# A two-layer hybrid token mixer on one core: scan products moved from GpSimd to VectorE, Mamba step sizes multiplied in at the outputs, and the last norm moved ahead of a branch

## The chip, the cores and the metric

The kernel runs on one core of a Trainium2 chip. The metric is device time in microseconds (us), from the start of one execution to its end. Five engines work beside each other, each with an instruction stream of its own that is executed in order: TensorE (PE, matrix products, with its weight loads shown as PEld), VectorE (DVE), ScalarE (ACT), GpSimd (POOL) and SyncE (SP), which here only issues DMA transfers. An instruction starts when those ahead of it on its engine have started or ended and the semaphores that it waits for have come.

## What is computed

256 latent and 256 context tokens of width 1024 pass through two layers. In each layer a normed and modulated input goes through one projection into three mixers that run side by side, a diagonal state-space scan (S5), a gated delta rule (GDN) and Mamba-2 (SSD), each in both directions; their outputs are concatenated and projected back. Then comes a dense SwiGLU (layer 0) or a top-2-of-8 mixture of experts (layer 1), and after layer 1 a last RMSNorm. The parts of the reference that the change touches, cut:

```python
# S5: h_t = lam * h_(t-1) + bu_t, complex, both directions
def _affine_combine(left, right):
    a_l, b_l = left
    a_r, b_r = right
    return a_l * a_r, a_r * b_l + b_r
# Mamba-2 inside a chunk: xdt = x * dt, and exp(cs_i - cs_j) for i >= j
y_diag = jnp.einsum("bncge,bnsge,bgjncs,bnsgjp->bncgjp", cc, bc, seg_decay(a_cs), xc)
y_off = jnp.einsum("bncge,bngjpe,bgjnc->bncgjp", cc, states[:, :-1], jnp.exp(a_cs))
...
y = xf * lax.rsqrt(jnp.mean(xf * xf, axis=-1, keepdims=True) + EPS)   # rmsnorm
```

## The kernel before

All matrix products of fp32 operands are made of three products of rounded parts: an operand is split into a high part H (ACT, line 321 for weights) and a remainder L (DVE, line 322), and PE sums hH·wH, hL·wH and hH·wL. So each weight tile costs a transfer, one ACT and one DVE instruction before PE can use it.

The source issues work in the order of the functions, and a scheduler then sets the order on each engine from priority bands (`self.band(...)`, with the numbers of the tables `Q0` for layer 0 and `Q1` for layer 1) and from the reuse of buffers in the pools. On the chip that order is fixed: an instruction that waits holds up all behind it on its engine, and a DMA that waits holds up all behind it on the SP queue.

In the mixer of a layer, the input projection runs on PE, and its tiles pass a convolution of four multiply-adds on DVE (`cv_acc`, line 800). Beside it stand, on DVE and POOL, the S5 scan (`s5_scan`: 11 levels over the 64 steps of the state `s5B`; for each piece two products `s5t` on POOL, line 609, and two additions on DVE, line 612), the remainders `wL` of the weights that are loaded, the GDN preparation (`gd_x`, `gd_prod`, and the iteration `iv_Q`, `iv_X` of lines 940 and 943) and the Mamba decays (`m2_decays`).

`m2_decays` makes, for four heads and one block of 128 tokens at a time (a quad; 16 quads in layer 0, 8 in layer 1), a 128x128 matrix for each head. `decay_quad` takes two `affine_select` on POOL (line 776), products on PE and one Exp on ACT (line 781), which give the decay `dq_W`. Lines 1070 and 1071 build `dq_E` = le·dt0 + ge·dt1 from the two triangles le and ge and the step sizes of the two directions, with one ACT and one DVE instruction for each head, POOL multiplies it with `dq_W` (line 1072), and line 1073 stores it to the scratch `WD` in DRAM. Later `m2` loads the matrices back as `m_E` (line 1161), multiplies them with the product B·C of that group from PSUM (line 1162) and uses them as moving operands on PE (`outs`, 12 calls in both layers together, two quads in each). The states of `m2` and the carried-in parts `m_yo` share one ring of buffers (`m2_xe`). `gate` norms the output (`m_sq`, `m_z`) and stores it to `yD`, from where `out_proj` reads it (`yr`, split into `yo`).

After the scan, `s5X` is stored to the scratch `XD` (line 626), on the same SP queue as the stores to `WD` and the loads for `m2`.

In the mixture of experts the main path computes all experts with up to 128 tokens each. `moe_rest` is a branch for experts with more tokens than that (a count `cnt` is loaded into registers on every engine, and the branch is not taken with these inputs). After the branch stands `final`, the last norm: squares on ACT, a sum over the features as eight products with a matrix of ones on PE, the reciprocal root (`rs_h`, `rs_y`, `rs_t`, `fr`), eight products `fy` shared out between DVE and POOL, and four DMAs.

Of the kernel before, what the change touches and what calls it, by code (L numbers as in the profile page):

```python
# [90 lines left out]
class Net:  # L91
# [968 lines left out]
    def m2_decays(self, p, sm, WD, first):  # L1060

        nc = self.nc
        for h0 in (0, 4, 8, 12):
            for t in range(first, 4):
                W = p.tile([128, 4, 128], F32, name="dq_W", bufs=2)
                self.decay_quad(p, sm, t, h0, W, "bg", 2)
                E = p.tile([128, 4, 128], F32, name="dq_E", bufs=2)
                for h in range(4):
                    dt = [sm["sp"][:, t, d * 20 + h0 + h:d * 20 + h0 + h + 1] for d in range(2)]
                    nc.scalar.activation(E[:, h], self.ge, AF.Copy, scale=dt[1])  # L1070
                    nc.vector.scalar_tensor_tensor(E[:, h], self.le, dt[0], E[:, h], op0=OP.mult, op1=OP.add)
# [923 lines left out]
```

## Time and profile before

| | before |
|---|---|
| time, median of 3 runs | 2540.91 us (2539.93 to 2543.95) |
| the profiled execution | 2542.29 us |
| its span in the trace | 2540.6 us |
| mean granted TensorE clock | 0.958 |
| PE busy | 2327.2 us (92%) |
| DVE busy | 1887.3 us (74%) |
| ACT busy | 1422.5 us (56%) |
| POOL busy | 377.0 us (15%) |

The profile is of one execution. Busy time is the time in which an engine executes instructions other than register, branch and DMA-issuing ones; it is an average over the whole span, in which the engines take turns at being the slowest. The 1.7 us between the execution's time and its span lie outside of the trace.

### The profile page before, as it was taken

What the parts mean: (1) busy time and instruction counts of PE and PEld (TensorE: products, weight loads), DVE (VectorE), ACT (ScalarE), POOL (GpSimd) and SP (SyncE); (2) the same over time, 40 slices, a digit from 0 to 9 for tenths busy, and PEclk for the clock granted to TensorE, in tenths of its full rate; (3) what the DMA queues carried; (4) which work ended last, traced back from release to release, by engine and by line L of the source; (5) the groups of instructions that cost most, each with busy time, mean ns of one, the idle gap of its engine ahead of it and who ended that gap; (6) DMA issues with size and microseconds to landing.
All of it is one profiled execution on the core that took longest, in us unless ns stands there. A gap on an engine that the chain in (4) does not pass through costs nothing. (4 is left out here: it accounts for less than half of the span.)

```text
span 2540.6 us, 36281 instructions
## 1 busy us (share of the span) xinstructions
PE 2327.2 (92%) x12886; PEld 1873.5 (74%) x12886; DVE 1887.3 (74%) x3035; ACT 1422.5 (56%) x2203; POOL 377.0 (15%) x435
## 2 busy tenths in 40 slices
PE   7999786889989999998988789789999999999997
PEld 4878665666757777886876667787887888888876
DVE  8787998446558674436578975568888888888886
ACT  4665476333234444235756653447777777676765
POOL 0011667312100000000046442100000000000000
PEclk9899997999989999998998899889999999999998
DMA  7444332986445656323443445387999999999993
GB/s 248 125 126 122 101 102 90 267 268 224 145 170 206 245 164 215 92 93 95 151 139 110 157 148 158 112 294 271 346 340 339 350 341 338 358 340 342 346 354 133
DMA packets 222378, 543.86 MB, mean 214 GB/s; under 512 B 25584, under 2 KB 105456, under 8 KB 186096
## 3 DMA queue, kind: packets, MB, share of 16 engines
q1 hardware_dynamic: 222192, 541.49, 62.0%
q8 instruction: 103, 1.69, 0.3%
q14 instruction: 83, 0.68, 0.1%
HBM read 487.87 MB, written 53.54 MB: 213 GB/s over the span
## 5 line engine op out<-in xcount | busy, mean ns | idle before, releaser
L1670 DVE TENSOR_TENSOR mwL<-mwr,mwH 128x2048 fp32r<-128x2048 f32 (+1 forms) x272 | 605.0, 2226 | 97.2 <-PE bank L162 59.1
L1669 ACT ACTIVATE mwH<-mwr 128x2048 fp32r<-128x2048 f32 (+1 forms) x272 | 508.1, 1868 | 204.6 <-PE bank L162 168.6
L321 ACT ACTIVATE wH<-wr 128x512 fp32r<-128x512 f32 (+2 forms) x388 | 233.1, 605 | 380.2 <-PE bank L162 261.5
L322 DVE TENSOR_TENSOR wL<-wr,wH 128x512 fp32r<-128x512 f32 (+2 forms) x388 | 279.9, 724 | 210.1 <-ACT wH L321 202.7
L162 PE MATMUL bank<-mwL,xeH 128*128 128x512 f32 (+1 forms) x768 | 292.6, 381 | 9.3 <-DVE mwL L1670 9.3
L162 PE MATMUL bank<-mwH,xeL 128*128 128x512 f32 (+1 forms) x768 | 288.1, 376 | 0.0
L162 PE MATMUL bank<-mwH,xeH 128*128 128x512 f32 (+1 forms) x768 | 284.7, 377 | 1.7 <-ACT mwH L1669 1.7
L162 PE MATMUL bank<-hH,wH 128*128 128x512 f32 (+2 forms) x656 | 249.1, 387 | 28.3 <-ACT cv_acc L798 15.2
L162 PE MATMUL bank<-hH,wL 128*128 128x512 f32 (+2 forms) x656 | 250.5, 382 | 14.3 <-DVE wL L322 14.3
L162 PE MATMUL bank<-hL,wH 128*128 128x512 f32 (+2 forms) x656 | 250.8, 383 | 1.1 <-DVE hL L300 1.1
L800 DVE SCALAR_TENSOR_TENSOR cv_acc<-cv_raw,pp,cv_acc 128x512 f32<-128x512 f32 (+1 forms) x192 | 164.9, 874 | 11.1 <-ACT cv_acc L796 5.8
L162 PEld LDWEIGHTS bank<-mwL,xeH 128*128 128x128 f32 x768 | 144.3, 188 | 37.7 <-DVE mwL L1670 11.7
L162 PEld LDWEIGHTS bank<-hH,wH 128*128 128x128 f32 (+1 forms) x656 | 127.2, 195 | 56.6 <-ACT cv_acc L798 17.1
L162 PEld LDWEIGHTS bank<-mwH,xeH 128*128 128x128 f32 x768 | 144.1, 188 | 31.5 <-ACT mwH L1669 2.5
L162 PEld LDWEIGHTS bank<-mwH,xeL 128*128 128x128 f32 x768 | 144.3, 188 | 26.2
L162 PEld LDWEIGHTS bank<-hH,wL 128*128 128x128 f32 (+1 forms) x656 | 127.8, 195 | 40.4 <-DVE wL L322 16.9
L162 PE MATMUL bank<-yo,wH 128*128 128x512 f32 (+1 forms) x512 | 134.0, 353 | 16.2 <-ACT yo L1385 12.1
L162 PEld LDWEIGHTS bank<-hL,wH 128*128 128x128 f32 (+1 forms) x656 | 127.7, 195 | 25.4 <-DVE hL L300 2.4
L162 PE MATMUL bank<-mwL,eaH 128*128 128x512 f32 x352 | 139.2, 396 | 0.0
L162 PE MATMUL bank<-fhH,wH 128*128 128x512 f32 x352 | 138.1, 396 | 0.9 <-ACT fa L1439 0.9
L162 PE MATMUL bank<-mwH,eaL 128*128 128x512 f32 x352 | 138.5, 394 | 0.0
L162 PE MATMUL bank<-fhL,wH 128*128 128x512 f32 x352 | 138.0, 392 | 0.0
(447 smaller groups left out, 4684.2 us busy)
## 6 DMA issues: line engine op xcount, KB each, us to landing
mwr<-in_moe_gu_dram SPq DMA_DIRECT2D x176, 1024.0 KB, 6.3
mwr<-in_moe_dn_dram SPq DMA_DIRECT2D x80, 1024.0 KB, 6.3
wr<-in_w_in_dram SPq DMA_DIRECT2D x160, 256.0 KB, 2.9
ada<-in_ada_w_dram SPq DMA_DIRECT2D x24, 1024.0 KB, 6.4
wr<-in_w_out_dram SPq DMA_DIRECT2D x64, 256.0 KB, 2.8
ada<-in_ada_w_dram SPq DMA_DIRECT2D x32, 512.0 KB, 6.5
wr<-in_ffn_w_gate_dram SPq DMA_DIRECT2D x44, 256.0 KB, 2.7
wr<-in_ffn_w_up_dram SPq DMA_DIRECT2D x44, 256.0 KB, 2.7
```

The costliest lines, as they stand in the source:

```text
L162: return self.nc.tensor.matmul(*a, **k)
L321: nc.scalar.activation(wH, w, AF.Copy)
L322: nc.vector.tensor_tensor(wL, w, wH.bitcast(F32), op=OP.subtract)
L800: nc.vector.scalar_tensor_tensor(acc, raw[:, :, j:j + 256], w[:, j:j + 1], acc, op0=OP.mult, op1=OP.add)
L1669: nc.scalar.activation(wH, w, AF.Copy)
L1670: nc.vector.tensor_tensor(wL, w, wH.bitcast(F32), op=OP.subtract)
```

## The change

It has three parts. In `s5_scan` the products move from POOL to DVE. `m2_decays` stops after the Exp and stores `dq_W` itself, with four buffers instead of two; `outs` takes over what it left out: B·C from PSUM is masked with le and ge into two SBUF tiles (which reuse the slices of B and C in `m_in`), and for each head ACT scales one with dt1, DVE adds the other times dt0, and DVE multiplies a quad with the loaded `m_W`. The product of B and C now stands behind the carried-in parts, and the quads `m_E` come from the ring `m2_xe`, which has five buffers instead of four. The last norm is called ahead of the branch, on tiles that the expert pool has already, with all eight products on DVE and a DMA behind every second one; inside the branch it is called once more.

```diff
@@ s5_scan
-                    nc.gpsimd.tensor_tensor(t[x], src[:, :, ::-1, :] if x else src,
+                    nc.vector.tensor_tensor(t[x], src[:, :, ::-1, :] if x else src,
                                             lam[:, e, x].unsqueeze(1).to_broadcast([128, m, 2, 32]), op=OP.mult)
@@ m2_decays
-                W = p.tile([128, 4, 128], F32, name="dq_W", bufs=2)
+                W = p.tile([128, 4, 128], F32, name="dq_W", bufs=4)
                 self.decay_quad(p, sm, t, h0, W, "bg", 2)
-                E = p.tile([128, 4, 128], F32, name="dq_E", bufs=2)
-                for h in range(4):
-                    dt = [sm["sp"][:, t, d * 20 + h0 + h:d * 20 + h0 + h + 1] for d in range(2)]
-                    nc.scalar.activation(E[:, h], self.ge, AF.Copy, scale=dt[1])
-                    nc.vector.scalar_tensor_tensor(E[:, h], self.le, dt[0], E[:, h], op0=OP.mult, op1=OP.add)
-                nc.gpsimd.tensor_tensor(E, E, W, op=OP.mult)
-                nc.sync.dma_start(WD[:, t, h0:h0 + 4], E)
+                nc.sync.dma_start(WD[:, t, h0:h0 + 4], W)
@@ m2, outs: behind the carried-in parts
-            psc = bank()
-            self.mm(psc[:, 0:128], BT, CT, start=True, stop=True)
...
+            psc = bank()
+            self.mm(psc[:, 0:128], BT, CT, start=True, stop=True)
+
+            nc.vector.tensor_tensor(BT, psc[:, 0:128], self.le, op=OP.mult)
+            nc.vector.tensor_tensor(CT, psc[:, 0:128], self.ge, op=OP.mult)
             E = []
             for q in range(2):
-                E.append(p.tile([128, 4, 128], F32, name="m2_E", bufs=Q[l]["b_E"]))
                 h0 = g * 8 + 4 * q
-                nc.sync.dma_start(E[q], WD[:, t, h0:h0 + 4])
-                nc.vector.tensor_tensor(E[q], psc[:, 0:128].unsqueeze(1).to_broadcast([128, 4, 128]), E[q], op=OP.mult)
+                W = p.tile([128, 4, 128], F32, name="m2_W", bufs=Q[l]["b_E"] - 1)
+                nc.sync.dma_start(W, WD[:, t, h0:h0 + 4])
+                E.append(p.tile([128, 4, 128], F32, name="m2_E", tag="m2_xe", bufs=Q[l]["b_xe"] + 1))
+                for h in range(4):
+                    dt = [sm["sp"][:, t, d * 20 + h0 + h:d * 20 + h0 + h + 1] for d in range(2)]
+                    nc.scalar.activation(E[q][:, h], CT, AF.Copy, scale=dt[1])
+                    nc.vector.scalar_tensor_tensor(E[q][:, h], BT, dt[0], E[q][:, h], op0=OP.mult, op1=OP.add)
+                nc.vector.tensor_tensor(E[q], E[q], W, op=OP.mult)
@@ moe, at its end
+        last = self.final_tiles(px[1][0], acc)
+        self.final(*last)
+        self.moe_rest(l, ab, ht, rk, gate, iota, cnt, last)
         px[1][1].close()
-        self.moe_rest(l, ab, ht, rk, gate, iota, cnt)
@@ final, new
+        for k in range(KT):
+            nc.scalar.activation(sq[:, k], self.xT[:, k], AF.Square)
+            self.mm(ps[:, :256], self.ones, sq[:, k], start=(k == 0), stop=(k == KT - 1))
+        self.rsqrt(None, r, ps[:, :256], [128, 256], 1.0 / D, tiles=tiles)
+        g = self.prm(0, "fng")
+        for k in range(KT):
+            nc.vector.scalar_tensor_tensor(y[:, k], self.xT[:, k], g[:, k:k + 1], r, op0=OP.mult, op1=OP.mult)
+            if k % 2 == 1:
+                nc.sync.dma_start(self.out.rearrange("(k p) t -> p k t", p=128)[:, k - 1:k + 1], y[:, k - 1:k + 1])
```

The order on the engines is the scheduler's, so it is shown here at three places, first of before and then of the change. A row is one instruction, or several alike in a row (xN).

The first place is DVE at the start of the scan of layer 0 (`s5B` the scan's additions, `s5t` its products, `cv_acc` the convolution, `wL` the remainders of weights, `gd_x` GDN's preparation). Before:

```order
L892 TENSOR_TENSOR gd_x_2930<-gd_x_2930,gd_prod_3080 128x16x15
L800 SCALAR_TENSOR_TENSOR cv_acc<-cv_raw,pp_72,cv_acc 128x512
L612 TENSOR_TENSOR s5B<-s5B,s5t 128x8x64 x2
L322 TENSOR_TENSOR wL<-wr,wH 128x512
L612 TENSOR_TENSOR s5B<-s5B,s5t 128x8x64
L800 SCALAR_TENSOR_TENSOR cv_acc<-cv_raw,pp_72,cv_acc 128x512
L612 TENSOR_TENSOR s5B<-s5B,s5t 128x8x64
L800 SCALAR_TENSOR_TENSOR cv_acc<-cv_raw,pp_72,cv_acc 128x512
L322 TENSOR_TENSOR wL<-wr,wH 128x512
L892 TENSOR_TENSOR gd_x_2935<-gd_x_2935,gd_prod_3085 128x16x15
L800 SCALAR_TENSOR_TENSOR cv_acc<-cv_raw,pp_72,cv_acc 128x512
L612 TENSOR_TENSOR s5B<-s5B,s5t 128x8x64
```

Of the change:

```order
L892 TENSOR_TENSOR gd_x_2930<-gd_x_2930,gd_prod_3080 128x16x15
L609 TENSOR_TENSOR s5t<-s5B,s5l 128x512 x3
L800 SCALAR_TENSOR_TENSOR cv_acc<-cv_raw,pp_72,cv_acc 128x512
L609 TENSOR_TENSOR s5t<-s5B,s5l 128x512
L892 TENSOR_TENSOR gd_x_2935<-gd_x_2935,gd_prod_3085 128x16x15
L612 TENSOR_TENSOR s5B<-s5B,s5t 128x8x64 x2
L322 TENSOR_TENSOR wL<-wr,wH 128x512
L800 SCALAR_TENSOR_TENSOR cv_acc<-cv_raw,pp_72,cv_acc 128x512
L612 TENSOR_TENSOR s5B<-s5B,s5t 128x8x64
L609 TENSOR_TENSOR s5t<-s5B,s5l 128x512
L612 TENSOR_TENSOR s5B<-s5B,s5t 128x8x64
L609 TENSOR_TENSOR s5t<-s5B,s5l 128x512
```

The products stand in pairs ahead of the additions that read them, among the same convolution steps and remainders.

The second place is the SP queue in layer 0 behind the scan (`WD` the store of a quad, `XD` that of the scan's result, `m_in` and `m_E` the first loads of `m2`, `ada` the modulation weights, whose source is the same size each time). Before:

```order
L1073 DMA WD_3090<-dq_E 128x512
L626 DMA XD_1897<-s5X 128x512
L1073 DMA WD_3090<-dq_E 128x512
L626 DMA XD_1897<-s5X 128x512 x4
L1073 DMA WD_3090<-dq_E 128x512
L626 DMA XD_1897<-s5X 128x512 x3
L1073 DMA WD_3090<-dq_E 128x512
L1161 DMA m_E<-WD_3090 128x512 x4
L1101 DMA m_in<-mD_94 128x4x128
L1103 DMA m_in<-mD_94 128x2x128
L1101 DMA m_in<-mD_94 128x4x128
L1103 DMA m_in<-mD_94 128x2x128
```

Of the change, from the last stores to `WD` on:

```order
L1067 DMA WD_3090<-dq_W 128x512 x3
L1335 DMA mD_94<-cvo 128x512
L1067 DMA WD_3090<-dq_W 128x512
L190 DMA ada<-in_ada_w_dram 128x4x256 x2
L1067 DMA WD_3090<-dq_W 128x512
L190 DMA ada<-in_ada_w_dram 128x4x256
L626 DMA XD_1897<-s5X 128x512
L190 DMA ada<-in_ada_w_dram 128x4x256
L626 DMA XD_1897<-s5X 128x512 x2
L190 DMA ada<-in_ada_w_dram 128x4x256
L626 DMA XD_1897<-s5X 128x512
L1335 DMA mD_94<-cvo 128x512
```

The last stores of quads stood among and behind those to `XD`, and now all 16 stand ahead of the first of these; loads of `ada` have come to stand between the stores to `XD`, and the first loads of `m2` stand 25 rows further down the queue than before.

The third place is PE in the output projection of layer 0 (`yo` its operand, `m_E` and `m_yo` the last outputs of `m2`, `m_sq` the sum of squares of its last `gate`). Before, the last `m_sq`:

```order
L162 MATMUL bank_6905<-yo,wH 128x512 x2
L162 MATMUL bank_6905<-yo,wL 128x512
L162 MATMUL bank_6905<-yo,wH 128x512 x2
L162 MATMUL bank_7001<-yo,wH 128x512 x2
L162 MATMUL bank_6905<-yo,wL 128x512
L162 MATMUL bank_6594<-m_sq,cst 128x256 x4
L162 MATMUL bank_7001<-yo,wL 128x512
L162 MATMUL bank_7001<-yo,wH 128x512 x2
L162 MATMUL bank_7001<-yo,wL 128x512
```

Of the change:

```order
L162 MATMUL bank_7040<-yo,wL 128x512
L162 MATMUL bank_7040<-yo,wH 128x512 x2
L162 MATMUL bank_7040<-yo,wL 128x512
L162 MATMUL bank_6538<-m_S_6293,m_in 128x512
L162 MATMUL bank_6571<-m_E,m_xt 64x128 x8
L162 MATMUL bank_6571<-cst,m_yo 128x128 x4
L162 MATMUL bank_6594<-m_sq,cst 128x256 x4
L162 MATMUL bank_6962<-yo,wH 128x512
L162 MATMUL bank_7001<-yo,wH 128x512
L162 MATMUL bank_7040<-yo,wH 128x512
L162 MATMUL bank_6962<-yo,wH 128x512
```

Of the 384 products with `yo`, 206 stood ahead of the last `m_sq`, and now 228 do; the last `m_E` and `m_yo`, which stood 138 instructions or more ahead of it, now stand directly before it.

## Rows read from the trace of the kernel before

**Rows 1.** The page: busy time by engine; DVE busy tenths in 40 slices.
```profile
PE 2327.2 (92%) x12886; PEld 1873.5 (74%) x12886; DVE 1887.3 (74%) x3035; ACT 1422.5 (56%) x2203; POOL 377.0 (15%) x435
...
DVE  8787998446558674436578975568888888888886
```

**Rows 2.** Busy time by stretch: us, each engine, TensorE clock, DMA share.
```profile
430.00:480.00 50.00, 39.46 (x265) 30.01 (x263) 27.11 (x48) 35.85 (x81) 23.52 (x22) 0.86 0.67 208
480.00:530.00 50.00, 40.97 (x348) 29.11 (x344) 26.04 (x55) 13.59 (x37) 16.18 (x15) 0.96 0.97 279
...
1500.00:1580.00 80.00, 73.43 (x568) 58.30 (x567) 42.89 (x83) 24.02 (x60) 19.80 (x17) 1.00 0.61 170
1760.00:2500.00 740.00, 729.76 (x3510) 601.79 (x3509) 641.45 (x410) 535.67 (x398) 0.00 (x0) 1.00 0.93 345
```

**Rows 3.** DVE by group, 283 to 417 us: xcount | busy, mean ns | idle.
```profile
L800 DVE SCALAR_TENSOR_TENSOR cv_acc<-cv_raw,pp,cv_acc 128x512 f32<-128x512 f32 x42 | 48.1, 1151 | 0.1
L612 DVE TENSOR_TENSOR s5B<-s5B,s5t 128x512 f32<-128x512 f32 x20 | 25.5, 1279 | 0.1
L1071 DVE SCALAR_TENSOR_TENSOR dq_E<-cst,sp,dq_E 128x128 f32<-128x128 f32 x36 | 23.1, 685 | 0.0
L322 DVE TENSOR_TENSOR wL<-wr,wH 128x512 fp32r<-128x512 f32 x19 | 22.9, 1210 | 0.0
...
L940 DVE TENSOR_TENSOR iv_Q<-bank,cst 128x512 f32<-128x512 f32 x8 | 5.3, 677 | 0.0
```

**Rows 4.** POOL by group, the same stretch.
```profile
L609 POOL TENSOR_TENSOR s5t<-s5B,s5l 128x512 f32<-128x512 f32 x22 | 35.6, 1634 | 8.5 <-DVE s5B L612 8.5
L776 POOL TENSOR_SCALAR_AFFINE_SELECT dq_r<-la 128x1024 fp32r<-128x1024 f32 x20 | 28.1, 1415 | 0.6 <-PE bank L162 0.6
L1072 POOL TENSOR_TENSOR dq_E<-dq_E,dq_W 128x512 f32<-128x512 f32 x9 | 13.9, 1550 | 4.7 <-ACT dq_W L781 3.2 <-issue 1.4
```

**Rows 5.** Timeline of DVE around 1320 us: start, duration (of all xN).
```profile
1317.82 3.44 DVE L322 TENSOR_TENSOR wL<-wr,wH 128x512 fp32r<-128x512 f32 x2
...
1323.28 0.68 DVE L612 TENSOR_TENSOR s5B<-s5B,s5t 128x512 f32<-128x512 f32 x1
1323.88 0.68 DVE L322 TENSOR_TENSOR wL<-wr,wH 128x512 fp32r<-128x512 f32 x1
```

**Rows 6.** Timeline of POOL at the same time.
```profile
1313.94 6.77 POOL L609 TENSOR_TENSOR s5t<-s5B,s5l 128x512 f32<-128x512 f32 x4
```

**Rows 7.** Timeline of DVE at 462 us, POOL quiet.
```profile
462.30 1.17 DVE L1071 SCALAR_TENSOR_TENSOR dq_E<-cst,sp,dq_E 128x128 f32<-128x128 f32 x4 [0.28 <-ACT dq_E L1070]
```

**Rows 8.** Timeline of DVE at 451 us; in brackets its idle time before.
```profile
451.21 0.61 DVE L1071 SCALAR_TENSOR_TENSOR dq_E<-cst,sp,dq_E 128x128 f32<-128x128 f32 x2 [8.46 <-issue]
```

**Rows 9.** Timeline of the SP queue at 442 us.
```profile
442.79 6.74 SPq L626 DMA_DIRECT2D XD<-s5X  x3
```

**Rows 10.** ACT by group, 283 to 435 us: the scalings of the decays.
```profile
L1070 ACT ACTIVATE dq_E<-cst,sp 128x128 f32<-128x128 f32 x44 | 14.1, 400 | 20.8 <-DMA WD<-dq_E 11.0 <-DVE gd_x L892 9.7
```

**Rows 11.** DVE by group, layer 1, 1299 to 1437.5 us.
```profile
L322 DVE TENSOR_TENSOR wL<-wr,wH 128x512 fp32r<-128x512 f32 x45 | 43.3, 969 | 13.0 <-ACT wH L321 13.0
...
L612 DVE TENSOR_TENSOR s5B<-s5B,s5t 128x512 f32<-128x512 f32 x22 | 25.5, 1167 | 0.1
```

**Rows 12.** DVE, the decay matrices of layer 1, 1300 to 1500 us.
```profile
L1071 DVE SCALAR_TENSOR_TENSOR dq_E<-cst,sp,dq_E 128x128 f32<-128x128 f32 x32 | 18.8, 637 | 0.0
```

**Rows 13.** PE waits of 640 to 770 us: total, times, longest.
```profile
PE bank L162 <- ACT yo L1385: 7.9, 1, 7.9
```

**Rows 14.** Timeline of the tail, three of its rows.
```profile
2518.30 3.22 DVE L1773 SCALAR_TENSOR_TENSOR xT<-bank,mods,xT 128x256 f32<-128x256 f32 x8
...
2521.60 2.56 ACT L1865 ACTIVATE fsq<-xT 128x256 f32<-128x256 f32 x8 [2.34 <-DVEq L1779]
...
2524.18 6.49 PE L162 MATMUL bank<-fsq,cst 128*128 128x256 f32 x16 [4.23 <-ACT fsq L1865]
```

**Rows 15.** Busy time by stretch, where the last norm sums its squares.
```profile
2524.00:2528.00 4.00, 3.82 (x9) 3.15 (x10) 0.00 (x0) 2.64 (x5) 0.00 (x0) 0.50 0.02 4
```

More of the change, by code (lines that the diff above doesn't have):

```diff
@@ L1118, in states @@
                         continue
-                    w = p.tile(s8, F32, name="m2_xe", tag="m2_xe", bufs=Q[l]["b_xe"])
+                    w = p.tile(s8, F32, name="m2_xe", tag="m2_xe", bufs=Q[l]["b_xe"] + 1)
                     nc.vector.tensor_tensor(w, v8(px), hb(sm["dde"][:, d, t, hs]), op=OP.mult)
@@ L1617, in gather @@
         nc = self.nc
-        xH, xL = [p.tile([128, KT, 2, 128], F32R, name=f"xe{x}") for x in "HL"]
+        xH, xL = [p.tile([128, KT, 2, 128], F32R, name=f"xe{x}", tag=f"xe{x}") for x in "HL"]
         yield xH, xL
@@ L1773, in moe_add, with moe_rest @@
         self.nc.vector.scalar_tensor_tensor(x, y, self.mods[l][:, 40 + m, 0:1], x, op0=OP.mult, op1=OP.add)
-    def moe_rest(self, l, ab, hts, rk, gate, iota, cnt):
+    def moe_rest(self, l, ab, hts, rk, gate, iota, cnt, last):
         nc, tc, A = self.nc, self.tc, self.A
@@ L1837, in moe_rest @@
                             nc.vector.tensor_tensor(sg, pg[1], sg, op=OP.mult)
-                            wd = p.tile([128, D], F32, name="r_wd", bufs=2)
+                            wd = p.tile([128, D], F32, name="r_wd")
                             for half in range(2):
@@ L1845, in moe_rest @@
                                         stop=(f == FF // 128 - 1))
-                        yv = p.tile([128, D], F32, name="r_yv")
+                        yv = p.tile([128, D], F32, name="r_yv", tag="r_xe")
                         for half in range(2):
@@ L1857, in moe_rest, with final_tiles, final @@
                         nc.vector.tensor_scalar(ec, ec, 1.0, None, op0=OP.add)
-    def final(self):
-        nc, tc = self.nc, self.tc
-        with tc.tile_pool(name="fin", bufs=1) as p:
-            ps = self.ps("mm")
-            for k in range(KT):
-                sq = p.tile([128, 256], F32, name="fsq", bufs=KT)
-                nc.scalar.activation(sq, self.xT[:, k], AF.Square)
-                self.mm(ps[:, :256], self.ones, sq, start=(k == 0), stop=(k == KT - 1))
-            r = p.tile([128, 256], F32, name="fr")
-            self.rsqrt(p, r, ps[:, :256], [128, 256], 1.0 / D)
-            y = p.tile([128, KT, 256], F32, name="fy")
-            g = self.prm(0, "fng")
-            xg = p.tile([128, 3, 256], F32, name="fxg")
-            for i in range(3):
-                nc.scalar.activation(xg[:, i], self.xT[:, 2 * i + 1], AF.Copy, scale=g[:, 2 * i + 1:2 * i + 2])
-            for k in range(KT):
-                if k in (1, 3, 5):
-                    nc.gpsimd.tensor_tensor(y[:, k], xg[:, k // 2], r, op=OP.mult)
-                else:
-                    nc.vector.scalar_tensor_tensor(y[:, k], self.xT[:, k], g[:, k:k + 1], r, op0=OP.mult, op1=OP.mult)
-            for k0 in range(0, KT, 2):
-                nc.sync.dma_start(self.out.rearrange("(k p) t -> p k t", p=128)[:, k0:k0 + 2], y[:, k0:k0 + 2])
+            self.final(*last)
+    def final_tiles(self, p, acc):
+        y = p.tile([128, KT, 256], F32, name="fy", tag="xeH")
+        t = p.tile([128, KT, 256], F32, name="fr", tag="xeL")
+        return acc, t[:, 0], y, [t[:, i] for i in (1, 2, 3)]
+    def final(self, sq, r, y, tiles):
+        nc = self.nc
+        ps = self.ps("mm")
+        for k in range(KT):
[7 more added lines that the diff above has]
+                nc.sync.dma_start(self.out.rearrange("(k p) t -> p k t", p=128)[:, k - 1:k + 1], y[:, k - 1:k + 1])
     def run(self):
@@ L1900, in run @@
             self.moe(1)
-            self.final()
 @with_exitstack
```

4 lines of the change are left out of this document (2 added, 2 removed).

## The prediction

> **What bounds the kernel now.** I read the page first: PE is busy for 92% of the span and DVE for 74%, but DVE's slices reach 8 and 9 in tenths around slices 5 to 7 [rows 1], so the two take turns. The table by stretch then tells where. In the experts (1760 to 2500 us) PE is busy for 729.8 of 740 us and POOL for none [rows 2]; nothing of the change touches that stretch but its start and its end, so I let it keep its length and move as a whole. The change lives in three places: the scan stage of each layer, the Mamba outputs behind it, and the tail.
>
> In the scan stage of layer 0 (283 to 417 us) I took the groups of DVE with shapes kept apart. Their idle column is near zero: DVE is the bound. But look at the means [rows 3]. A convolution step, an addition of the scan and a weight remainder, all of 512 columns, take 1.15, 1.28 and 1.21 us, whereas `iv_Q`, which reads PSUM and one SBUF tile, takes 0.68. The timelines say why. While POOL runs four products from 1313.94 to 1320.71 [rows 6], a remainder takes 1.72 us; when POOL has just stopped, an addition takes 0.68 and the next instruction starts 0.60 behind it [rows 5]. So each large POOL operation delays one DVE instruction with two SBUF inputs by about 1 us, and DVE spends much of this stage waiting for POOL. The Trainium skill, "SBUF — State Buffer", section "SBUF: two separate sides", gives a rule for it: VectorE and GpSimd share one pair of ports as an exclusive lock, taken by GpSimd's operations and by VectorE's with two SBUF inputs, and the other one blocks. By that rule the trace agrees, with 0.68 us alone and 1.72 beside POOL.
>
> **Scan products, layer 0.** At their own price (0.60 for 512 columns, 0.29 for a `dq_E` step of 128 [rows 7]) the stage's DVE work is 42 convolution steps 25.2, 36 `dq_E` 10.4, 19 remainders 11.4, the scan's additions about 16 (20 of 512, 14 shorter ones at some 4), 16 of the iteration 9.6, others 2.5: 75 us. The stretch lasts 134, so 59 are lost to POOL, which ran about 56 large operations there (22 of `s5t`, 20 selects, 9 `dq_E` [rows 4], and 5 others): 1.05 us each. The change takes 22 `s5t` and 9 `dq_E` off POOL, which leaves 25: 26 lost. DVE loses 10.4 of `dq_E`, gains 38 products, 22×0.60 and 16 shorter ones at about 5, together 18.4, and the four additions that came behind this stretch, 2.3. So 75 − 10.4 + 18.4 + 2.3 + 26 = 111 against 134, or −23. POOL, with less to do, may run more of its 32 selects inside the stretch (12 more cost 12). I take −18, bounds −25 and −10.
>
> **The stall behind it.** At 451.21 DVE had been idle for 8.46 us ahead of a `dq_E` step [rows 8]. The row names no releaser, but the code does: the step follows an ACT scaling into the same `dq_E`, whose two buffers come free with their stores, and the stores stand behind the three of `XD`, whose issue takes 6.7 us [rows 9]. The change has no `dq_E`, and its order puts every store of a quad ahead of `XD`. I take −9, bounds −9 and 0, since the first loads of `m2` still queue behind `XD`, and loads of `ada` now stand between.
>
> **Mamba outputs.** Each of the 12 calls of `outs` (8 in layer 0) gets eight DVE steps at 0.29 [rows 7], two masks, whose nearest row is that of such a step, so 0.6, and eight ACT scalings; the two products `m_E` stay in number. That is 2.9 us of DVE a call, 23 in layer 0 and 12 in layer 1. Their cover is DVE's idle time: it is busy for 27.1 and 26.0 of 50 us behind the scan [rows 2] and for 42.9 of 80 in layer 1. With half of each engine's time free, but in order behind waits, I take a fifth of the first and two fifths of the second, +5 in each layer; bounds 0 and +10. If that cover were gone, it would be the full 23 and 12.
>
> A rule that speaks against this part comes from the same section of the skill: `m_E` used to read PSUM and now reads two SBUF tiles, so GpSimd can block it. The trace bounds it: 24 products by at most 1.05 are 25 us, but POOL is busy for only 16.2 of 50 us there [rows 2], which makes it some 8, and most of that falls in idle time. My sum stays by the row and puts nothing for it; by the rule alone it would be 8 higher.
>
> **Output projection, layer 0.** The last outputs now stand 22 products of `yo` deeper on PE, directly ahead of `m_sq`. PE waited 7.9 us for the last `yo` [rows 13], which goes through `gate`, a store and a load. With `m_sq` 22 products later, at 0.21 us each (as in the experts, 729.8 us for 3510 [rows 2]), 5 us of cover are gone, and the last outputs' own chain delays them by as much again. I take +10, bounds 0 and +15. What is late next is the norm ahead of the dense SwiGLU.
>
> **Layer 1.** From 1299 to 1437.5 the same means show: 45 remainders at 0.97, 22 additions at 1.17 [rows 11]. Over their own 0.69 that is 12.6 and 10.6, and with the convolution and short additions some 35 us lost. About 28 of some 40 large POOL operations are `s5t`, so 27 come back, and 18.4 of products are added: −9; the 13 us that DVE idles for ACT's `wH` [rows 11] let some of them hide. I take −12, bounds −18 and −8. Behind it the decays' 32 DVE steps, 18.8 us [rows 12], leave a stretch in which DVE is the bound, but their work returns at the outputs: −8, bounds −16 and 0.
>
> **The tail.** The last eight `moe_add` take DVE from 2518.30 to 2521.52; only then, behind the branch, ACT squares, and PE starts at 2524.18 after 4.23 us of idleness [rows 14], at a granted clock of 0.50, its lower level [rows 15], for 6.49 us. Ahead of the branch each square follows its own addition (0.40 apart; ACT keeps up, at 0.32 each), so PE may start at about 2519.5 and end between 2523.5, soon behind the last square, and 2526.5 if the clock has fallen: 4.2 to 7.2 earlier. On DVE eight products instead of five cost 3×0.4, in part under the DMAs. The branch's own loads and jumps now stand behind the output DMAs and end before these land. I take −6.5, bounds −8 and −4.
>
> **Sum.** Layer 0: −18 − 9 + 5 + 10 = −12. Layer 1: −12 − 8 + 5 = −15. Tail −6.5. Together −33.5 on 2542.3 of the profiled execution, which is 1.4 above the median of the runs, so about 2507 as a median. With all bounds on one side it would be −76 or +13.
>
> **Rivals.**
> - *Later waits take it back.* The scan stage gets shorter, but the output projection waits for GDN and for `ada` (DMA share 0.97 in 480 to 530 [rows 2]), so of layer 0's −27 nothing stays, and layer 1 keeps half of its −20: with its +5 about −5, the tail −6.5, layer 0 about 0: 2529.
> - *More is won.* DVE's idle time covers all of the outputs, nothing is late on PE: −27 − 20 − 6.5 = −53.5, at the outer bounds −76: about 2480.
> - *Slower: the serial chain at the outputs.* Each call goes mask, then eight times ACT and DVE in turn, then `m_E`. An ACT scaling takes 0.40 [rows 10]. Eight of them 3.2, the masks 0.6, the last DVE step 0.3 and the last `m_E` 0.7 make 4.8 us, where a call had 1.3 before, and about half as much again comes on top where the next ACT or DVE instruction stands behind other work in order: 6 us more. All 12 bare are +72, against the −53.5 of the other parts with +10 on PE: 2570. It decides from (53.5 − 10)/12 = 3.6 us more a call. Against it: PE is busy for 39.5 and 41.0 of 50 us there and has GDN's and S5's work beside.
> - *Slower: VectorE is simply full.* "Perfetto Trace Analysis", section "Optimizing Scalar/DVE Operations", of the Trainium skill says that with VectorE saturated, offloading to ScalarE or even GpSimd may make sense; it adds that the shared port may spoil this. If POOL's operations cost DVE nothing, the 18.4 us of each layer would lengthen both stages: +37 − 10 − 9 for `dq_E` + 10 + 10 − 6.5 = +31: 2572. The 1.72 beside 0.68 us [rows 5] speaks against it.
> - *No change*: only the tail shows, and one late wait in layer 0 eats it.
>
> **How the numbers follow.** The forecast (2490 to 2524) 0.52, more is won 0.15, taken back 0.18, no change 0.04, the chain 0.08, VectorE full 0.03. The likeliest gives 2507. Eight in ten lie between 2478 and 2537: the upper end takes in the case that the waits take it back, the lower one that half of the cases of more won that lies next to the forecast. A run of this kernel tells 0.2%, or 5 us, from no change; faster by more than that 0.85, within 0.04, slower 0.11.
>
> **What would show it.** Of the changed kernel: convolution steps and remainders of the scan stages near 0.8 us instead of 1.15 and 1.21, with POOL's share there halved, and the last scan addition of layer 0 some 20 us earlier; no DVE idleness of 8 us ahead of the first states of `m2`; the last `yo` waited for by some 15 us on PE; the eight sums of the last norm ending 4 to 7 us behind the last addition. The prediction is wrong if the means of the scan stage stay above 1 us (then something other than POOL delays DVE), if GDN's iteration starts earlier and its end does not, or if PE waits for `m_E` or DVE for ACT's scaling by more than 3.6 us a call.

## The result, and the profile after

The changed kernel takes 2505.01 us (median of 4 runs, 2504.33 to 2511.89), against 2540.62 before (4 runs, 2539.93 to 2543.95): a ratio of 0.9864, with a 95% interval of 0.9846 to 0.9882. That is 35.6 us less, where 33.5 were forecast. A second measurement beside experiments gave 0.9869 (0.9847 to 0.9891). The profiled execution took 2504.33 us, its span 2502.6.

The page of the changed kernel, with the lines that answer to [rows 1]:

```profile
PE 2310.1 (92%) x12886; PEld 1857.5 (74%) x12886; DVE 1867.7 (75%) x3138; ACT 1419.4 (57%) x2200; POOL 255.3 (10%) x332
...
DVE  8887995577458674336578966678888888888887
```

POOL has lost a third of its work (377.0 to 255.3 us), DVE has about as much as before. The stretches of [rows 2], at the same times of the clock, so with other work in them:

```profile
430.00:480.00 50.00, 45.78 (x386) 34.33 (x384) 30.22 (x61) 16.88 (x49) 14.64 (x14) 1.00 0.94 271
480.00:530.00 50.00, 45.94 (x369) 31.98 (x370) 30.79 (x76) 22.85 (x70) 7.09 (x6) 0.90 0.98 290
...
1760.00:2460.00 700.00, 689.86 (x3330) 569.18 (x3329) 606.85 (x390) 506.40 (x378) 0.00 (x0) 1.00 0.93 345
```

The experts run as before (PE busy for 98.6% of the stretch). Layer 0's m2 and GDN are now in 430 to 480, with PE at 45.8 of 50 us where it had 39.5.

DVE by group in the scan stage of layer 0, from the first product (278.9) to the last convolution step (397), in answer to [rows 3], and POOL's largest group of the same stretch, in answer to [rows 4]:

```profile
L800 DVE SCALAR_TENSOR_TENSOR cv_acc<-cv_raw,pp,cv_acc 128x512 f32<-128x512 f32 x41 | 39.5, 972 | 0.0
L612 DVE TENSOR_TENSOR s5B<-s5B,s5t 128x512 f32<-128x512 f32 x22 | 21.7, 990 | 0.0
L322 DVE TENSOR_TENSOR wL<-wr,wH 128x512 fp32r<-128x512 f32 x19 | 18.4, 969 | 0.0
L609 DVE TENSOR_TENSOR s5t<-s5B,s5l 128x512 f32<-128x512 f32 x22 | 18.1, 845 | 0.0
L940 DVE TENSOR_TENSOR iv_Q<-bank,cst 128x512 f32<-128x512 f32 x8 | 5.4, 677 | 0.0
```

```profile
L776 POOL TENSOR_SCALAR_AFFINE_SELECT dq_r<-la 128x1024 fp32r<-128x1024 f32 x32 | 53.0, 1677 | 9.6 <-PE bank L162 9.0 <-DVE gd_x L892 0.3 <-POOL cv_raw L791 0.3
```

The three means fell from 1.15, 1.28 and 1.21 us to 0.97, 0.99 and 0.97, and not to 0.8: all 32 selects of the layer ran in this stage, where 20 did before. `iv_Q`, which reads PSUM, stays at 0.68. POOL's share of the stage fell from 78% to 57%, and not to half (before, then the change; columns as in [rows 2]):

```profile
283.30:415.70 132.40, 91.21 (x407) 72.56 (x405) 132.19 (x152) 71.85 (x141) 102.93 (x95) 0.85 0.28 91
278.90:397.10 118.20, 92.91 (x451) 72.69 (x450) 118.16 (x156) 67.33 (x114) 67.08 (x60) 0.91 0.36 119
```

Where the gain was given back shows in PE's waits from 600 to 760 us, in answer to [rows 13]:

```profile
PE bank L162 <- ACT yo L1387: 11.9, 1, 11.9
PE bank L162 <- DVE m_E L1164: 4.5, 2, 4.2
PE bank L162 <- ACT m_sq L1189: 3.6, 1, 3.6
```

20.0 us where there were 7.9 for `yo` and 0.4 for `m_E`. The timeline of DVE at the last outputs of layer 0 tells the rest:

```profile
665.98 0.28 DVE L1152 TENSOR_TENSOR m_in<-bank,cst 128x128 f32<-128x128 f32 x1
...
669.99 1.88 DVE L1163 SCALAR_TENSOR_TENSOR m_E<-m_in,sp,m_E 128x128 f32<-128x128 f32 x5 [0.47 <-ACT m_E L1162]
...
673.29 0.69 DVE L1164 TENSOR_TENSOR m_E<-m_E,m_W 128x512 f32<-128x512 f32 x1
677.20 1.12 DVE L1177 SCALAR_TENSOR_TENSOR m_in<-m_in,pp,bank 128x128 f32<-128x128 f32 x4 [3.22 <-PE bank L162]
684.70 0.42 DVE L263 TENSOR_SCALAR m_sq<-bank 128x256 f32<-128x256 f32 x1 [6.37 <-PE bank L162]
...
687.12 1.67 DVE L1196 SCALAR_TENSOR_TENSOR m_z<-m_z,pp,m_sq 128x256 f32<-128x256 f32 x4
696.49 2.48 DVE L1388 TENSOR_TENSOR yo<-yr,yo 128x1024 fp32r<-128x1024 f32 x2 [7.69 <-ACT yo L1387]
```

Mask, steps, `m_E`, the update of `m_in`, the norm, its store and load, and `yo`: 30 us in a row, in which DVE and PE are mostly idle (busy for 10.7 and 11.0 of the 31 us from 666 to 697). And the tail, in answer to [rows 14]:

```profile
2486.14 3.22 DVE L1777 SCALAR_TENSOR_TENSOR xT<-bank,mods,xT 128x256 f32<-128x256 f32 x8
...
2486.65 3.16 ACT L1875 ACTIVATE xT<-xT 128x256 f32<-128x256 f32 x8 [1.21 <-DVE xT L1777]
...
2487.63 3.62 PE L162 MATMUL bank<-xT,cst 128*128 128x256 f32 x16
2491.28 0.42 DVE L263 TENSOR_SCALAR fr<-bank 128x256 f32<-128x256 f32 x1 [1.93 <-PE bank L162]
...
2493.63 3.25 DVE L1880 SCALAR_TENSOR_TENSOR fy<-xT,pp,fr 128x256 f32<-128x256 f32 x8
```

The eight sums begin 1.49 us behind the first addition and end 1.9 us behind the last one. They take 3.62 us where they took 6.49, at the higher of the two levels of the granted clock (columns as in [rows 2]):

```profile
2487.60:2491.30 3.70, 3.65 (x18) 2.88 (x16) 1.77 (x6) 2.21 (x6) 0.00 (x0) 1.00 0.00 0
```

Three lengths, worked out from the traces. Each begins at the start of the layer's first product of the scan. They run to the end of the last step of the convolution, to the start of the last product of the output projection in layer 0, and to the end of the last scaling of GDN's output `gd_o` on POOL in layer 1:

| us | before | change | scan alone (E1) | Mamba alone (E2) | no scan (E6) | m2 first (E5) | no step sizes (E8) | no selects (E9) |
|---|---|---|---|---|---|---|---|---|
| layer 0, scan to last convolution | 132.4 | 118.2 | 140.1 | 121.3 | 121.2 | 118.7 | 118.2 | 111.4 |
| layer 0, scan to end of projection | 464.3 | 456.3 | 459.4 | 465.4 | 465.5 | 437.0 | 432.1 | 422.4 |
| layer 1, scan to end of GDN | 342.0 | 329.1 | 346.6 | 341.5 | 338.1 | 324.8 | 321.9 | 335.1 |

Two more profiles show how far such entries can be trusted. E3 leaves both layers as before and has 132.4, 468.0 and 343.6 in the three rows; E10 is the change again and has 118.3, 453.3 and 329.1. So an entry of the second row differs by 3 to 4 us between two profiles of the same instructions, and what layer 0 gained is 8 us by the one pair and 15 by the other.

From the start of the last weight remainder of the experts (`mwL`, 2513.00 before, 2480.85 after) to the end of the span it is 27.6 us before and 21.8 after. With the tail as before it is 25.3 in E1's profile and 27.2 in E2's, with the new one 21.5 in E3's. A single profile also holds swings of the granted clock that have nothing to do with the change. The largest is here, before and after, in a stretch ahead of everything that the change touches (columns as in [rows 2]):

```profile
85.00:100.00 15.00, 15.00 (x65) 13.31 (x64) 5.95 (x14) 7.89 (x18) 1.48 (x7) 0.51 0.17 70
```

```profile
85.00:100.00 15.00, 15.00 (x99) 12.53 (x97) 9.34 (x21) 12.12 (x25) 1.61 (x9) 0.91 0.22 88
```

At 0.51, the lower of the two levels, the same PE work took 5.4 us longer; in the profiles of the nine kernels below that have this stretch the clock is 0.89 to 1.00 there. So the two spans differ by 38.0, of which 5.4 are this; the medians, each over several runs, are what counts.

### The profile page after: what moved, and what is told of

It reads as the page before. It is cut to its first block, busy times and chain, and to the rows that moved or that the text cites. A ratio compares the mean times of both kernels' runs of the same rounds, so it can differ in the third digit from the quotient of the medians.

```text
span 2502.6 us, 36223 instructions
## 1 busy us (share of the span) xinstructions
PE 2310.1 (92%) x12886; PEld 1857.5 (74%) x12886; DVE 1867.7 (75%) x3138; ACT 1419.4 (57%) x2200; POOL 255.3 (10%) x332
## 4 chain that ended last, share of the span: by engine, by line
PE 63%; DVE 7%; ACT 5%; DMA 4%; issue 4%; POOL 0%; SPq 0%; DVEq 0%; ACTq 0%; POOLq 0%
PE bank L162 61%; DMA ada<-in_ada_w_dram 1%; DVE wL L322 1%; ACT mwH L1673 1%; DVE mwL L1674 1%; PE bank L1761 1%; DMA wr<-in_w_in_dram 1%; DVE cv_acc L800 1%; DMA s5D<-KD 1%; DVE s5B L612 1%; DMA s5V<-VD 0%; ACT s5X L623 0%; DVE s5t L609 0%; DVE nm_m L293 0%; PE bank L933 0%
## 5 line engine op out<-in xcount | busy, mean ns | idle before, releaser
L322 DVE TENSOR_TENSOR wL<-wr,wH 128x512 fp32r<-128x512 f32 (+2 forms) x388 | 264.9, 685 | 207.0 <-ACT wH L321 196.7
L800 DVE SCALAR_TENSOR_TENSOR cv_acc<-cv_raw,pp,cv_acc 128x512 f32<-128x512 f32 (+1 forms) x192 | 154.1, 818 | 12.4 <-ACT cv_acc L796 5.8
L162 PE MATMUL bank<-mwH,eaH 128*128 128x512 f32 x352 | 137.4, 395 | 0.5 <-ACT eaH L1765 0.5
```

The source lines that it names most:

```text
L162: return self.nc.tensor.matmul(*a, **k)
L322: nc.vector.tensor_tensor(wL, w, wH.bitcast(F32), op=OP.subtract)
L800: nc.vector.scalar_tensor_tensor(acc, raw[:, :, j:j + 256], w[:, j:j + 1], acc, op0=OP.mult, op1=OP.add)
```

## The experiments

The theory: a large POOL operation holds up a DVE instruction with two SBUF inputs; taking such operations off POOL shortens the stages that DVE sets, although DVE gets the products; the rest of the change costs a little at the outputs and in layer 0's projection. Against it stood that DVE is full (then the products' move costs 18.4 us a layer), and that the serial chain at the outputs decides. E1 to E3 were made first, one part of the change each, on the kernel before.

**E1, the scan alone.**

```diff
-                    nc.gpsimd.tensor_tensor(t[x], src[:, :, ::-1, :] if x else src,
+                    nc.vector.tensor_tensor(t[x], src[:, :, ::-1, :] if x else src,
```

> The kernel before with the scan's products on DVE and nothing else of the change. Theory (each large POOL operation holds up one DVE instruction with two SBUF inputs by about 1 us): each layer loses 28 large POOL products at about 1.05 us and gains 18.4 us of DVE work, so the scan stage is 8 to 11 us shorter a layer; in layer 0 much of it is given back at the output projection, where the order has the last m_sq behind 228 products of yo here too. About 2529 us. Rival (POOL costs DVE nothing, DVE is full): two times +18.4 us in the scan stages, 2565 or more.

2532.04 us, ratio 0.9970 (0.9957 to 0.9982): faster, so DVE is not simply full, but by 7.7 us and not by the price of the products. The groups of this run, from 279 to 421 us, say why:

```profile
L800 DVE SCALAR_TENSOR_TENSOR cv_acc<-cv_raw,pp,cv_acc 128x512 f32<-128x512 f32 x42 | 43.5, 1048 | 0.8 <-ACT cv_acc L798 0.8
L1071 DVE SCALAR_TENSOR_TENSOR dq_E<-cst,sp,dq_E 128x128 f32<-128x128 f32 x64 | 32.3, 546 | 0.0
```

```profile
L776 POOL TENSOR_SCALAR_AFFINE_SELECT dq_r<-la 128x1024 fp32r<-128x1024 f32 x32 | 44.0, 1390 | 17.6 <-PE bank L162 16.7 <-DVE cv_acc L800 0.9
L1072 POOL TENSOR_TENSOR dq_E<-dq_E,dq_W 128x512 f32<-128x512 f32 x16 | 28.8, 1797 | 27.0 <-ACT dq_W L781 9.0 <-DVE dq_E L1071 5.7 <-PE bank L162 4.2
```

POOL's free time was taken by its other work at once. All 64 steps of `dq_E`, 32 selects and 16 `dq_E` products now ran in the scan stage (36, 20 and 9 before), the stage got 8 us longer, and only what had been taken out of the time behind it was won. In layer 1 the last step of the convolution came 8 us earlier, as expected (it ends 172.8 us behind the first product, before 180.5), but the end of GDN did not (346.6 us, against 342.0 before and 343.6 in E3).

**E2, the Mamba part alone** (the hunks of `m2_decays` and `m2`).

> The kernel before with the Mamba part alone (the decays store their exponentials, the step sizes come in at the outputs). Theory: layer 0's scan stage loses nine dq_E products on POOL (9 us of DVE) and 36 DVE steps (10 us), layer 1's stretch behind the preparation about 8 us; the outputs cost some 10 of it again and the output projection of layer 0 some 10 more. About 2527 us. Rival (the serial chain at the outputs decides): each of the 12 calls costs 5 us or more, and the time is 2545 or more.

2533.03 us, ratio 0.9975 (0.9966 to 0.9985), 6.7 us. The scan stage of layer 0 is 11 us shorter, but the layer is not (table): its last outputs stand behind 228 products of `yo` here too, and PE waited 11.9, 3.6 and 3.5 us for `yo`, `m_sq` and `m_E`. The chain of 5 us a call does not decide.

**E3, the tail alone** (the hunks of `moe`, `moe_rest` and `final`).

> The kernel before with the last norm ahead of the branch and nothing else. Theory: squares behind their own additions and no idle PE ahead of the eight sums: 5 to 6.5 us less, 2535 us, all of it behind the last expert's last matrix product. Rival (the branch's instructions behind the output DMAs, and eight products on DVE, eat it): 2540.

2535.02 us, ratio 0.9987 (0.9978 to 0.9997), 4.7 us: the theory's side, a little less than it said. The interval reaches from 0.8 to 5.6 us, so the size is known only roughly.

**E6, all but the scan.** The three parts alone add up to some 19 us, and the change is worth 35.6. So the change was run with the products back on POOL.

```diff
-                    nc.vector.tensor_tensor(t[x], src[:, :, ::-1, :] if x else src,
+                    nc.gpsimd.tensor_tensor(t[x], src[:, :, ::-1, :] if x else src,
```

> The changed kernel with the scan's products back on POOL; the Mamba part and the tail stay. If the parts add up (scan alone -7.7, Mamba alone -6.7, tail alone -4.7), this is 2540 - 11 = 2529 us, and the products' move is worth 24 us beside the others though it was worth 8 alone: then the parts help each other. If instead the sum of the parts missed something of the Mamba part, this is near 2512 and the products' move is worth 8 here as well.

2527.23 us against 2541.49 of before in that measurement, ratio 0.9942 (0.9921 to 0.9963). The parts without the scan add up within the noise (14.3 us here, 11.4 alone); the products' move is worth some 20 us beside them and 8 alone. The length of the stage does not show why: it is 118.2 us in the change and 121.2 here. What differs is where POOL's selects of layer 0 run, here and then in the change (first and last start):

```profile
L776 POOL TENSOR_SCALAR_AFFINE_SELECT dq_r<-la x32: 1086/1366/1575, 293.5 to 423.6; 128x1024 fp32r<-128x1024 f32 x32
L776 POOL TENSOR_SCALAR_AFFINE_SELECT dq_r<-la x32: 1088/1536/3107, 282.1 to 392.3; 128x1024 fp32r<-128x1024 f32 x32
```

The last one starts 145.1 us behind the first product of the scan here, behind the stage, and 113.4 in the change, inside it. GDN's last product with `gd_o` starts at 337.8 here and at 315.1 in the change, and by the table the change is shorter by 9 us in either layer. So with the products and `dq_E` both gone, POOL is through with the decays before the stage ends, and GDN runs 23 us ahead. That the one brings the other is argued; no run separates them.

**E4, one more buffer for `m_in` in layer 0.**

```diff
-    wl=4, st_=4, yr=2, iv=5, b_in=4, b_xt=3, b_xe=4, b_E=4, mm=(0, 1), px=(2, 3, 4), bg=(5, 6, 7), ad=(7,), so=(6, 5),
+    wl=4, st_=4, yr=2, iv=5, b_in=5, b_xt=3, b_xe=4, b_E=4, mm=(0, 1), px=(2, 3, 4), bg=(5, 6, 7), ad=(7,), so=(6, 5),
```

> The changed kernel with five buffers m_in instead of four in layer 0 (b_in=5 in Q0). In the order this puts the last m_E and the last m_sq of layer 0 ahead of all 384 products of yo, where the change has 228 of them ahead. Theory (what the scan stage wins in layer 0 is given back in the output projection, because the last outputs stand too deep in PE's order): the waits for m_E, m_sq and the last yo, 19.7 us together, fall to less than 5, and the time to 2486 us or so. Rival (GDN's chain or the loads of ada set the end of the projection anyway): PE waits elsewhere just as long, 2502 to 2508 us.

2590.82 us, ratio 1.0202 (1.0188 to 1.0215): much slower, against both. The first states of `m2` start at 575.9 us, where the change has 442.3; from the program I take it that the larger pool found its place in SBUF only when other pools had gone (GDN's last product with `gd_o` starts at 566.2 us in this run, just ahead of these states). No run shows this by itself:

```profile
L1114 DVE TENSOR_TENSOR m_xe<-bank,dde x24: 673/683/692, 575.9 to 1613.1; 128x512 f32<-128x512 f32 x24
```

The whole of `m2` then stood bare at the end of the layer. This says nothing on the theory; E5 asks the same without memory.

**E5, Mamba first in layer 0.**

```diff
-    gd=1.0, gl=1.1, g1=2.0, xb=2.0, m2=4.0, yo0=1.06, yo1=1.0, yo2=1.67, yo3=5.0, parts=0, w=0.8, gdl=1.0, gdo=1.0,
-    m2o=3.9, m2g=4.0, qk=1.0, qq=1.0, qv=1.0, sm=1.0, gi1=1.12, gl3=1.12, sg=3.2, qo=(1, 0, 2), gx=0, wr=3, wh=4,
+    gd=1.0, gl=1.1, g1=2.0, xb=2.0, m2=0.9, yo0=1.06, yo1=1.0, yo2=1.67, yo3=5.0, parts=0, w=0.8, gdl=1.0, gdo=1.0,
+    m2o=0.9, m2g=0.9, qk=1.0, qq=1.0, qv=1.0, sm=1.0, gi1=1.12, gl3=1.12, sg=3.2, qo=(1, 0, 2), gx=0, wr=3, wh=4,
```

> The changed kernel with the three bands of the Mamba part in layer 0 (m2, m2o, m2g of Q0) at 0.9 instead of 4.0, 3.9 and 4.0, ahead of the output projection's 1.06 and 1.0; no buffer changes. In the order the last m_E then stands ahead of all 384 products of yo, and the last m_sq behind 26 instead of 228. Theory (the change's win in layer 0 is given back because the last outputs stand too deep on PE): the waits for the last m_E, m_sq and yo, 19.7 us with the change, fall under 6, and the time to about 2491 us. Rival (GDN's chain or the loads of ada set the end of the projection, and giving Mamba the first place only delays these): 2502 us or more.

2496.57 us against 2541.49, ratio 0.9823 (0.9794 to 0.9851). Its interval touches that of the change, but the profile shows the cause: layer 0 is 19 us shorter (437.0 to 456.3; 16 against the 453.3 of E10), and of the three waits there is left

```profile
PE bank L162 <- DVE m_E L1164: 5.7, 3, 4.1
...
PE bank L162 <- ACT m_sq L264: 1.8, 1, 1.8
```

with none for `yo`. These 7.5 us are more than the 6 that were said, and GDN's last product with `gd_o` starts 19 us later than in the change (334.2 against 315.1), as the rival had it. Some of the 19 us goes again up to layer 1's start, where the gain is 11. The theory holds in the main: part of what the scan stage won had been given back at the projection. The version is the fastest that keeps the computation. Whether the same bands would have helped the kernel before, without the change, was not tried.

**E7, the port by itself.** A kernel of its own, run once, which leaves out the whole computation: runs of DVE instructions of 128x512 with and without eight POOL operations beside them.

```python
STAGES = [(("sb", 12), ("mul", 0)), (("sb", 0), ("mul", 8)), (("sb", 0), ("sel", 8)), (("sb", 24), ("mul", 8)),
          (("ps", 24), ("mul", 8)), (("sb", 24), ("sel", 8)), (("ps", 24), ("sel", 8)), (("one", 24), ("mul", 8)),
          (("ps", 12), ("mul", 0)), (("one", 12), ("mul", 0))]
```

> A kernel of its own that leaves out the whole computation and measures the disputed price: DVE products of 128x512 with two SBUF inputs (12 alone, 24 beside 8 POOL products, 24 beside 8 POOL selects), with one PSUM and one SBUF input (12 alone, 24 beside either), and with one SBUF input alone (12 alone, 24 beside 8 POOL products). Theory (a DVE instruction with two SBUF inputs and a POOL operation exclude each other): 24 with two SBUF inputs take 14.4 us of their own and about 8 us more beside 8 products of 1.05 us, as long as POOL and DVE take turns, and as much more beside 8 selects; those with a PSUM input take 14.4 to 15 beside either. Rival (POOL costs DVE nothing, and the long means of the scan stage are waits for data): 14.4 us beside anything.

Its timeline of DVE (line 123: two SBUF inputs; 125: one PSUM and one SBUF; 127: one SBUF) and of POOL (116: products; 118: selects):

```profile
11.68 8.68 DVE L123 TENSOR_TENSOR d<-a,x 128x512 f32<-128x512 f32 x12
...
47.43 25.05 DVE L123 TENSOR_TENSOR d<-a,x 128x512 f32<-128x512 f32 x24
...
75.01 17.36 DVE L125 TENSOR_TENSOR d<-pb,a 128x512 f32<-128x512 f32 x24
...
94.89 23.66 DVE L123 TENSOR_TENSOR d<-a,x 128x512 f32<-128x512 f32 x24
...
121.06 17.36 DVE L125 TENSOR_TENSOR d<-pb,a 128x512 f32<-128x512 f32 x24
...
140.94 18.68 DVE L127 TENSOR_SCALAR d<-a 128x512 f32<-128x512 f32 x24
...
162.13 8.66 DVE L125 TENSOR_TENSOR d<-pb,a 128x512 f32<-128x512 f32 x12
...
173.25 5.50 DVE L127 TENSOR_SCALAR d<-a 128x512 f32<-128x512 f32 x12
```

```profile
22.37 11.02 POOL L116 TENSOR_TENSOR q<-a,x 128x512 f32<-128x512 f32 x8 [21.86 <-DVE a L109]
35.39 9.59 POOL L118 TENSOR_SCALAR_AFFINE_SELECT q<-a 128x1024 f32<-128x1024 f32 x8 [2.00 <-DVE a L109]
47.00 13.31 POOL L116 TENSOR_TENSOR q<-a,x 128x512 f32<-128x512 f32 x8 [2.01 <-DVE a L109]
74.57 11.04 POOL L116 TENSOR_TENSOR q<-a,x 128x512 f32<-128x512 f32 x8 [14.26 <-DVE a L109]
```

24 with two SBUF inputs would take 17.4 us alone (12 take 8.68); they take 25.05 beside eight products, 0.96 us more for each, and 23.66 beside eight selects, 0.79 more for each. With one operand in PSUM they take 17.36 beside either, as alone, and POOL its 11.04 us, as alone (11.02). So POOL holds DVE up, and it hangs on DVE's operands. The Trainium skill, "SBUF — State Buffer", section "SBUF: two separate sides", has the rule for two SBUF inputs: the engine that comes second blocks for the whole instruction of the other. The runs agree with the rule in the operands; of the 1.38 us that a product takes on POOL alone, DVE lost 0.96, and whether the rest fell into gaps of DVE's own stream no run separates. The last case went beyond the expectation: 24 instructions with a single SBUF input, which take 11.0 us alone (12 take 5.50), took 18.68 beside eight products.

**E8, the outputs without step sizes and masks.**

```diff
-            nc.vector.tensor_tensor(BT, psc[:, 0:128], self.le, op=OP.mult)
-            nc.vector.tensor_tensor(CT, psc[:, 0:128], self.ge, op=OP.mult)
...
-                for h in range(4):
...
-                nc.vector.tensor_tensor(E[q], E[q], W, op=OP.mult)
+                nc.vector.tensor_tensor(E[q], psc[:, 0:128].unsqueeze(1).to_broadcast([128, 4, 128]), W, op=OP.mult)
```

> The changed kernel with the step sizes and the two masks left out at the outputs: m_W times the product of B and C from PSUM is used as it is, so the two masks, eight ACT scalings and eight DVE steps of each call are gone (what it computes lacks the step sizes). Measures what the added work at the outputs costs. Theory (most of it lies beside other work; the prediction put +5 in each layer and part of the +10 of the projection on it): 12 to 18 us less than the change, 2490 us. Rival (the serial chain at the outputs is bare): 12 calls by 5 us, 2445 us. Other rival (all of it is hidden): 2505 us.

2478.61 us, ratio 0.9765 (0.9741 to 0.9789), against 2506.20 and 0.9869 of the change beside it: the added work at the outputs costs 27.6 us, well above what was said. By the table it is 24 in layer 0 (432.1 to 456.3) and 7 in layer 1 (321.9 to 329.1), some of which goes again elsewhere; over the 12 calls it is 2.3 each, and not the chain's 5. Not all of it is the work: without it the order has the last `m_E` behind 206 products of `yo`, where the change has 228.

**E9, the decays with one pair of selects in each layer.**

```diff
+            if keep is not None and d in keep:
+                r = keep[d]
+            else:
                 r = p.tile([128, 8, 128], F32R, name="dq_r", bufs=bufs)
...
+                if keep is not None:
+                    keep[d] = r
...
+        keep = {}
...
-                self.decay_quad(p, sm, t, h0, W, "bg", 2)
+                self.decay_quad(p, sm, t, h0, W, "bg", 2, keep)
```

> The changed kernel with only the first pair of selects of the decays in each layer; the other quads reuse these two tiles (what it computes has wrong decays), so 30 selects on POOL go in layer 0 and 14 in layer 1, and no DVE instruction. Theory (each large POOL operation holds up DVE by some 0.8 us where DVE is the bound): the scan stage of layer 0 ends some 20 us earlier and the decays' stretch of layer 1 some 10, of which layer 0 gives half back at its projection: about 2485 us. Rival (POOL costs DVE nothing): 2505 us.

2483.99 us, ratio 0.9782 (0.9759 to 0.9805), 22 us less than the change, though no DVE instruction has gone. From 278 to 366 us:

```profile
L612 DVE TENSOR_TENSOR s5B<-s5B,s5t 128x512 f32<-128x512 f32 x22 | 17.9, 824 | 0.0
...
L322 DVE TENSOR_TENSOR wL<-wr,wH 128x512 fp32r<-128x512 f32 x18 | 13.5, 750 | 2.3 <-ACT wH L321 2.3
```

The remainders are at 0.75, the scan is done 31 us earlier. Work on POOL costs DVE time; that is shown here inside the kernel. How much of the 22 us is DVE's time, and how much comes from decays that are done earlier, is not separated. Most of it was won in layer 0 (422.4 against 456.3); layer 1 gave some back.

**E10, the change once more.**

> The changed kernel once more, unchanged, beside the two kernels above on the same chip: 2505 us again, ratio 0.986, and no dip of the granted clock at 85 to 100 us, where only the profile of the kernel before has one.

2506.20 us, ratio 0.9869 (0.9847 to 0.9891), and 0.92 in the stretch from 85 to 100 us.

## Why the prediction was right, point by point

**Scan products, layer 0:** the mechanism held (E7, E9). The stage shrank by 14.2 us, within the bounds of 10 and 25; taken was 18. The select count fits as the reason: 32 in the stage, as the bound had it, and not 20. Most of the term is the Mamba part: alone it shortens the stage by 11.1 (E2), and the products' move adds 3 to that (E6). The sum's own items say the same, with 4.7 for the products (22 at 1.05 off, 18.4 on). What the sum had missed is that the products' move does not act by itself. Alone it made the stage longer (E1), since POOL's decays came forward. And beside the other parts it is worth some 20 us, most of it not in the stage's length but in GDN, which runs ahead (E6); for that the sum had no item.

**The stall:** the 8.46 us ahead of `dq_E` are gone with that step, but the term's use was smaller. The first states of `m2` start 12.6 us earlier, counted from the scan, and not the 27 of both terms; loads for S5 and of `ada` stand on SP ahead of those of `m2`. GDN ends 36 us earlier. The sign that DVE would have no idleness of 8 us there did not come true: it waits for PE instead, in GDN's iteration.

```profile
414.01 0.69 DVE L940 TENSOR_TENSOR iv_Q<-bank,cst 128x512 f32<-128x512 f32 x1 [10.05 <-PE bank L162]
```

**Mamba outputs and output projection:** the steps were right and their size was off. Together they were put at 15 us in layer 0, and cost 24 (E8); at 5 in layer 1, and cost 7. The last `yo` was waited for by 11.9 us, where "some 15" was said, and `m_E` and `m_sq` by 8.1 more. The working had read the order wrongly: it put the last outputs 22 products of `yo` deeper, which is right for `m_sq` (206 to 228), but the last `m_E` went from behind 26 products to behind 228. Counted from the scan, its products end up 28 us later (last start 367.7 before, 395.8 in the change), and the slack of 45 us that they had ahead of `m_sq` shrank to 9. Moving it ahead (E5) and leaving the work out (E8) each take most of the cost back, 19 and 24 us, so place and work are not separated: the late place lays the added steps bare. So layer 0 as a whole won 8 us (464.3 to 456.3; 15 by the profiles of E3 and E10), and 11 up to the start of layer 1 (15), where 12 were forecast. Larger gains in front (24.2 + 8 = 32 or more, where 27 had been put) met larger costs; that the total came so near is in part luck.

By the rule of the Trainium skill that `m_E`, now with two SBUF inputs, can be blocked, 8 us would have been put on it. Its 16 instances from 430 to 700 us took 0.680 us on average, as `iv_Q` does, so the row-based sum, which put nothing, was right; POOL is busy for 14.6 and 7.1 of 50 us there.

**Layer 1:** 12.9 us to the end of GDN (14.5 by E3 and E10), where 15 were forecast. **The tail:** 5.8 us in the profiles and 4.7 alone, where 6.5 were. The sums end 1.9 us behind the last addition, where the sign said 4 to 7; the working's own times (2523.5 to 2526.5, against a last addition at 2521.52) had said 2 to 5.

**Signs of being wrong:** the means of the stage stayed under 1 us, but only just (0.97 to 0.99). GDN's end came earlier with its iteration. PE waited for `m_E` by 6.7 us and DVE for ACT's scaling by 3.4 over all 12 calls together, far from 3.6 a call, though a single wait reached 4.2.

**Rivals.** That later waits take it back was true of layer 0 in part; the added work at the outputs costs 2.3 us a call (24 over the 8 calls of layer 0, so 3.0 there), below the 3.6 from which the chain would have decided; that VectorE is simply full is refuted by E1, E7 and E9. What was argued and not shown: that SP's order delays the first states of `m2`, how the emptier POOL brings GDN forward, and how E9's layer 1 gave back time.

## What to carry to other kernels

Before moving work off a busy VectorE to GpSimd, look at the operands: where VectorE's instructions read two SBUF tiles, each GpSimd operation beside them takes some of its time from VectorE (0.8 to 1.0 us in E7), and a product that takes 1.4 us there and 0.6 to 0.7 here is cheaper here. But a freed engine is filled by whatever its queue has next, so two such changes may be worth more together than apart; test the parts in both directions, each alone and each left out. And after a stage has got shorter, look in the order at what stands in front of the last consumer: a priority set for the old lengths (4.0 against 1.06 here) may now put the end of the longest chain behind work that could wait. And take a second profile before you explain a few microseconds of one stage.

## What the runs showed of the hardware that was not expected

A DVE instruction with one SBUF input of fp32 (0.46 us for 512 columns alone) is held up by POOL's products too: 24 of them took 18.68 us instead of 11.0. POOL's own delay is smaller: eight products took 11.02 us alone and 13.31 beside DVE. The section of the Trainium skill that is named at E7 counts VectorE's two-port modes among the operations that take the lock. That this instruction runs in one would fit its 0.46 us, against 0.72 with two inputs, but no run shows the mode. And one more buffer of 3 KB a partition cost 86 us (E4); that it did so by when its pool could open is taken from the program.
